# Down products by quadrants, and weight sums by adding transfers, in a two-layer hybrid on one core

## The chip, the cores and the metric

The kernel runs on one core of one Trainium2 chip. A core has TensorE (PE in the profile), VectorE (DVE), ScalarE (ACT), GpSimd (POOL) and SyncE (SP), each with its own in-order instruction stream. The metric is the device time of one execution in microseconds, the median over the runs. The profile is of one execution.

## The reference

Two layers over 512 tokens of width 1024. The first layer mixes by chunked spatial gating and memory attention, the second by forgetting attention and memory attention; each is followed by a gated feed-forward block, which is what the change touches. D_FF is 2816, that is 22 tiles of 128 hidden rows.

```python
def rmsnorm(x, g):
    xf = x.astype(jnp.float32)
    y = xf * lax.rsqrt(jnp.mean(xf * xf, axis=-1, keepdims=True) + RMS_EPS)
    return (y * g.astype(jnp.float32)).astype(x.dtype)
...
for layer in range(DEPTH):
    ...
    h = h + rmsnorm(mixed @ w_out[layer], ln_mix_post[layer])
    f = rmsnorm(h, ln_ffn_pre[layer])
    f = (jax.nn.silu(f @ w_ffn_gate[layer]) * (f @ w_ffn_up[layer])) @ w_ffn_down[layer]
    h = h + rmsnorm(f, ln_ffn_post[layer])
```

Everything is float32.

## The kernel before, in words

**Three matmuls for one product.** A float32 operand is split into a high part (a cast on ScalarE to float32r, line 239) and a low part (a subtraction on VectorE, line 240). `mm3` (line 180) then multiplies high by high, high by low and low by high into the same PSUM tile; these are the lines 182 to 184 of the profile. So every weight tile costs one cast on ScalarE and one subtraction on VectorE (`split`) before TensorE can use it. The parts lie in a ring of eight buffers for high and eight for low parts (`pair_of_parts`, line 123), each of 512 columns.

**Gate and up products.** The hidden row tiles are worked off in pairs. For a pair, `Seven` computes the gate (and then the up) rows of both tiles for all 512 tokens as one 2 by 2 product of blocks: two row tiles by two halves of the depth, times two halves of the depth by two halves of the tokens. Seven block products take the place of eight (the Winograd form of Strassen's scheme). One such `Seven` is called a set here: two weight loads of 512 KB into two of four `raw` buffers of 1024 columns, four sums of 512 columns on VectorE in place (lines 1022 to 1027), seven splits, seven products of twelve 256-column matmuls each (84 matmuls), and evacuations of `x`, `p` and `q` from PSUM into `s1` and `s2` by ScalarE copies (lines 1040 to 1055) and VectorE additions (1060, 1061, 1063). The gate's rows are multiplied by the inverse norm and go through Silu (1110, 1111); the up rows are multiplied by the gate (1116, 1118) and split into `fhi` and `flo`, the form in which the down products read them. The token side was combined and split once, ahead of the loop.

**PSUM.** Gate sets use the three banks of tag `mm`, up sets the three banks of `lg`, so that two sets can overlap.

**Down products.** Row tiles 0 and 1 are computed and multiplied by the down weights first. The other 20 go in four groups, (2 to 8), (8 to 14), (14 to 18) and (18 to 22). After the sets of a group come its down products: for each half `dh` of the 1024 outputs, four PSUM tiles (one per 128 tokens) are accumulated over the group's row tiles, with the hidden rows as the stationary side and 512 weight columns moving, and are then added into the sums `ys` by VectorE (line 1174). For four row tiles this is 4 x 2 x 4 x 3 = 96 matmuls. The last group's down products belong to the tail of the layer (`tail_of`), where the norm is formed.

**Order.** The kernel is written with a tile framework that orders each engine's instructions by its own estimates and takes care of buffers and semaphores. `behind(*last_sum)` ties instructions of a block behind the last evacuations of the set before (the two entries of `last_sum`), on the engine of each. SyncE issues the weight loads in its own order and waits for a free buffer ahead of each load. GpSimd computes the few reciprocal roots and some masks, and issues four small transfers between the layers.

The changed parts are `Seven`, `sevens` (which runs the two sets of a pair), and the loop of `feed_forward`. The core of the loop before:

```python
for dh in range(2):
    outs = [ps("mm" if tb < 2 else "lg", s="y") for tb in range(TB)]
    for kp in range(nk // 2):
        with behind(*(last_sum if dh + kp else ())):
            w = down_weights(layer, k0 + 2 * kp, dh)
```

## Time and profile before

| | |
|---|---|
| median of 3 runs | 1113.62 us (1113.4 to 1114.18) |
| span of the profiled execution, first to last instruction | 1111.4 us |
| TensorE busy | 1100.8 us (99%), 7382 matmuls |
| VectorE busy | 893.7 us (80%), 1735 instructions |
| ScalarE busy | 660.5 us (59%), 1397 instructions |
| GpSimd busy | 25.3 us (2%) |
| transfers | 118.12 MB, mean 106 GB/s |
| mean granted TensorE clock | 0.998 |

The profiled execution's own time is not listed beside its span; the span is 2.2 us below the median of the runs. In the profile's rows, `out<-in` names the tile written and the tiles read, without buffer numbers; `x` is a count; after the bar stand busy microseconds and the mean nanoseconds of one. Matmul records overlap: a matmul's recorded length is longer than the distance to the next one's start, so times per matmul are read from starts. The same holds, to a lesser degree, for VectorE and ScalarE. `PEclk` is the granted clock in tenths.

### The profile page before, as it was taken

How to read it: one execution, taken by the hardware profiler on the slowest of the kernel's cores; microseconds unless marked ns; L12 is line 12 of the kernel's file. 1: busy time of each engine (PE TensorE's matmuls, PEld its weight loads, DVE VectorE, ACT ScalarE, POOL GpSimd, SP SyncE). 2: the span in 40 equal slices, each digit the busy share in tenths (PEclk: the TensorE clock that was granted, in tenths of full speed). 3: DMA queues.
4: the chain of work that ended last, by engine and by line, in shares of the span. 5: the costliest groups of instructions: out<-in, count | busy, mean ns of one | idle time of the engine just before them, and what ended most of it. 6: DMA issues, size and time to landing. Idle time of an engine off the chain costs nothing.

```text
span 1111.4 us, 19500 instructions
## 1 busy us (share of the span) xinstructions
PE 1100.8 (99%) x7382; PEld 1000.1 (90%) x7382; DVE 893.7 (80%) x1735; ACT 660.5 (59%) x1397; POOL 25.3 (2%) x42
## 2 busy tenths in 40 slices
PE   9999999999999999999999999999999999999997
PEld 7998889998899898998988898889999899899996
DVE  8889658997697597896987898858997697687875
ACT  8776468664365264577665667668665265254553
POOL 0100000000000000001000000000000000000000
PEclk9999999999999999999999999999999999999999
DMA  7522322334133323343322654422224133333222
GB/s 267 162 76 77 98 74 76 115 109 141 57 112 97 117 92 114 97 148 117 104 88 62 173 132 116 131 76 74 79 90 154 62 114 96 101 109 114 77 76 76
DMA packets 64421, 118.12 MB, mean 106 GB/s; under 512 B 5260, under 2 KB 40088, under 8 KB 64328
## 3 DMA queue, kind: packets, MB, share of 16 engines
q1 hardware_dynamic: 63720, 116.18, 33.4%
q8 instruction: 58, 0.95, 0.4%
q0 software_dynamic: 192, 0.52, 0.2%
q14 instruction: 35, 0.29, 0.1%
q10 hardware_dynamic: 416, 0.18, 0.1%
HBM read 104.71 MB, written 2.10 MB: 96 GB/s over the span
## 4 chain that ended last, share of the span: by engine, by line
PE 94%; ACT 3%; DVE 1%; issue 1%; POOL 0%; DMA 0%; POOLq 0%; DVEq 0%; ACTq 0%
PE y L182 10%; PE y L183 10%; PE y L184 10%; PE a L182 5%; PE a L184 5%; PE a L183 5%; PE x L184 3%; PE e L182 3%; PE e L184 3%; PE e L183 3%; PE x L183 3%; PE x L182 3%; PE ps L184 3%; PE ps L183 3%; PE ps L182 3%; PE v L182 2%
## 5 line engine op out<-in xcount | busy, mean ns | idle before, releaser
L239 ACT CAST whi<-raw 128x512 fp32r<-128x512 f32 x460 | 273.1, 620 | 217.7 <-PE y L184 89.1
L240 DVE TENSOR_TENSOR wlo<-raw,whi 128x512 fp32r<-128x512 f32 x460 | 303.5, 684 | 69.5 <-ACT whi L239 67.8
L182 PE MATMUL y<-whi,fhi 128*128 128x512 f32 (+1 forms) x356 | 140.2, 394 | 0.4 <-DVE y L838 0.4
L184 PE MATMUL y<-whi,flo 128*128 128x512 f32 (+1 forms) x356 | 139.3, 391 | 0.0
L183 PE MATMUL y<-wlo,fhi 128*128 128x512 f32 (+1 forms) x356 | 139.2, 391 | 0.0
L184 PE MATMUL x<-xshi,wlo 128*128 128x256 f32 x320 | 89.9, 281 | 0.0
L182 PE MATMUL a<-xshi,whi 128*128 128x256 f32 x320 | 89.8, 281 | 0.0
L183 PE MATMUL x<-xslo,whi 128*128 128x256 f32 x320 | 89.7, 280 | 0.0
L182 PE MATMUL x<-xshi,whi 128*128 128x256 f32 x320 | 89.7, 280 | 0.0
L183 PE MATMUL a<-xslo,whi 128*128 128x256 f32 x320 | 89.7, 280 | 0.0
L184 PE MATMUL a<-xshi,wlo 128*128 128x256 f32 x320 | 89.6, 280 | 0.0
L184 PEld LDWEIGHTS y<-whi,flo 128*128 128x128 f32 x356 | 66.8, 188 | 15.7
L182 PEld LDWEIGHTS y<-whi,fhi 128*128 128x128 f32 x356 | 66.8, 188 | 15.6 <-DVE y L838 0.7
L183 PEld LDWEIGHTS y<-wlo,fhi 128*128 128x128 f32 x356 | 66.9, 188 | 14.7
L182 PEld LDWEIGHTS a<-xshi,whi 128*128 128x128 f32 x320 | 60.2, 188 | 0.5
L183 PEld LDWEIGHTS a<-xslo,whi 128*128 128x128 f32 x320 | 60.2, 188 | 0.3
L184 PEld LDWEIGHTS x<-xshi,wlo 128*128 128x128 f32 x320 | 60.3, 188 | 0.0
L183 PEld LDWEIGHTS x<-xslo,whi 128*128 128x128 f32 x320 | 60.2, 188 | 0.0
L184 PEld LDWEIGHTS a<-xshi,wlo 128*128 128x128 f32 x320 | 60.2, 188 | 0.0
L182 PEld LDWEIGHTS x<-xshi,whi 128*128 128x128 f32 x320 | 60.2, 188 | 0.0
L183 PE MATMUL ps<-xslo,whi 128*128 128x256 f32 x192 | 53.9, 283 | 0.6 <-DVE xslo L240 0.6
L184 PE MATMUL ps<-xshi,wlo 128*128 128x256 f32 x192 | 54.4, 285 | 0.0
(297 smaller groups left out, 3111.1 us busy)
## 6 DMA issues: line engine op xcount, KB each, us to landing
raw<-in_w_gate SPq DMA_DIRECT2D x44, 512.0 KB, 3.5
raw<-in_w_up SPq DMA_DIRECT2D x44, 512.0 KB, 3.6
raw<-in_w_down SPq DMA_DIRECT2D x44, 512.0 KB, 3.8
raw<-in_w_out SPq DMA_DIRECT2D x16, 512.0 KB, 4.8
raw<-in_w_b_q SPq DMA_DIRECT2D x8, 512.0 KB, 3.4
raw<-in_w_a_u SPq DMA_DIRECT2D x6, 512.0 KB
raw<-in_w_v SPq DMA_DIRECT2D x6, 512.0 KB, 4.3
raw<-in_w_k SPq DMA_DIRECT2D x6, 512.0 KB
```

What stands on the lines that cost most here:

```text
L182: PE.matmul(o, w[0], x[0], start=start, stop=False, skip_group_check=more)
L183: PE.matmul(o, w[0], x[1], start=False, stop=False, skip_group_check=more)
L184: return PE.matmul(o, w[1], x[0], start=False, stop=stop, skip_group_check=more)
L239: last_hi[0] = A.copy(hi, src)
L240: last_split[0] = last_hi[0], (eng or V).tensor_sub(lo, src, hi)
```

## The change

**Down products as seven.** The groups become (2, 6), (6, 10), (10, 14), (14, 18) and (18, 22). In the first four, that is for 16 of the 22 row tiles, the down product of four row tiles is computed as two 2 by 2 block products (one for each pair of row tiles), summed in PSUM: two row tiles by two halves of the outputs, times two halves of the tokens by two row tiles. The seven products `p`, `q` and `x` are accumulated over both pairs and given out to the quadrants of `ys` by fourteen additions (`give`); `p` is accumulated further after some of its values were given out. `seven_forms` forms the combinations of hidden rows that the products need. Each `Down` loads its weights into two `raw` buffers and a fourth quarter in `a22`, and takes seven splits and two sums. The half `dh = 1` of `ys` is held with its sign turned (`scale=1.0 - 2 * dh`, `turned_sign`).

**Place.** The down products of a group no longer follow its last set. They are kept in `pending` and run after the gate set of the next group's first pair, ahead of that pair's up set; the loads of that up set are issued ahead of the last down product (`ahead`). They use all six banks of `mm` and `lg`.

**Sums by adding transfers.** A set of gate or up weights used to load two times 512 KB and form four sums on VectorE. Now `both` gets the left halves of the two weight tiles, and a transfer from GpSimd's queue adds the whole second tile onto it (`accum_op=ALU.add`), which gives two of the four sums. The other two stay on VectorE. The fourth quarter comes by a load of its own into `a22`. The first three sets of a layer are made without the adding transfer (`adding = m + n > 4`). `Down` uses the same device. A set's seven products are ordered 1, 7, 6, 2, 5, 4, 3 in place of 1, 7, 2, 6, 4, 3, 5, and product 3 accumulates into `p` (but not in the first pair, `late`), so that the last 512-column sum from PSUM becomes one of 256 columns.

```diff
@@ tail_of
-                V.tensor_add(y, o[:, cols], y)
-                junk = temp("sq", (P, T), "sq", 3, BF16)
+                (V.tensor_sub if turned_sign and dh else V.tensor_add)(y, o[:, cols], y)
+                junk = temp("sq", (P, T), "sq", 1, BF16)
@@ class Seven
-        def __init__(self, xs, src, tag, rows):
-            self.xs, self.rows = xs, rows
-            w1, w2 = loaded(src(0)), loaded(src(1))
-            self.a = [w[:, d : d + 512] for w in (w1, w2) for d in (0, 512)]
...
+        def __init__(self, xs, w, m, tag, rows, adding=True, late=False):
+            self.xs, self.tag, self.rows, self.adding, self.late = xs, tag, rows, adding, late
+            raw, both = raw_tile(), raw_tile()
+            self.a11, self.a12 = raw[:, :512], raw[:, 512:]
+            self.s3, self.t = both[:, :512], both[:, 512:]
+            self.a22 = temp("a22")
+            if adding:
+                nc.sync.dma_start(both.rearrange("p (a c) -> p a c", a=2),
+                                  w[m : m + 2, :, :512].rearrange("a p c -> p a c"))
+                nc.sync.dma_start(raw, w[m])
+                G.dma_start(both, w[m + 1], accum_op=ALU.add)
+            else:
+                nc.sync.dma_start(raw, w[m])
+                nc.sync.dma_start(self.s3, w[m + 1, :, :512])
+            nc.sync.dma_start(self.a22, w[m + 1, :, 512:])
@@ sums
-            self.s3 = temp("s3")
-            V.tensor_add(self.s3, a11, a21)
-            self.w1 = self.parts(a11)
-            V.tensor_add(a21, a21, a22)
-            self.w2 = self.parts(a12)
-            V.tensor_add(a11, a21, a11)
-            V.tensor_add(a12, a11, a12)
+            if not self.adding:
+                V.tensor_add(self.t, self.s3, self.a22)
+                V.tensor_add(self.s3, self.a11, self.s3)
+            self.w1 = self.parts(self.a11)
+            self.w2 = self.parts(self.a12)
+            V.tensor_add(self.a11, self.t, self.a11)
+            V.tensor_add(self.a12, self.a11, self.a12)
@@ run
             elif what == 2:
                 self.product(self.x[:, left], self.w2, 2)
+                if not self.late:
+                    V.tensor_add(s1[:, left], self.x[:, left], s1[:, left])
...
             elif what == 3:
-                self.product(self.x[:, right], self.parts(a12), 5)
+                self.product(self.p, self.parts(self.a12), 5, True)
+                last_sum[0] = A.copy(s1[:, right], self.p)
             elif what == 4:
-                self.product(self.q, self.parts(a22), 4, True)
+                self.product(self.q, self.parts(self.a22), 4, True)
+                last_sum[1] = V.tensor_add(s2[:, left], self.q, s2[:, left])
             elif what == 5:
-                self.product(self.p, self.parts(a21), 6, True)
-                last_sum[0] = A.copy(s1[:, right], self.p)
+                self.product(self.p, self.parts(self.t), 6, True)
+                A.copy(s1[:, right], self.p)
+                V.tensor_add(s2[:, right], s1[:, right], s2[:, right])
@@ sevens
+                if n and pending:
+                    pending.pop()()
                 u = make()
                 u.sums()
-                for n in (1, 7, 2, 6, 4, 3, 5):
+                for n in (1, 7, 6, 2, 5, 4, 3):
                     u.run(n)
@@ new
+    def seven_forms(u0, u1, room):
...
+        t = temp("t3", tag="acc", bufs=2)
+        V.tensor_sub(t[:, left], u1[:, right], u0[:, right])
+        V.tensor_sub(u0[:, right], u0[:, left], u0[:, right])
+        pairs = [(act("fhi"), act("flo")) for _ in range(3)]
+        split(u0, *pairs[0])
+        split(u1, *pairs[1])
+        V.scalar_tensor_tensor(out=t[:, right], in0=u0[:, right], scalar=-1.0, in1=u1[:, right],
+                               op0=ALU.mult, op1=ALU.subtract)
+        split(t, *pairs[2])
+        V.scalar_tensor_tensor(out=u1[:, left], in0=t[:, right], scalar=-1.0, in1=u1[:, left],
+                               op0=ALU.mult, op1=ALU.subtract)
+        split(u1[:, left], *room)
...
+    class Down:
+        def __init__(self, layer, k, forms):
...
+            for x in range(2):
+                nc.sync.dma_start(view(both, x), part(x, 0))
+            nc.sync.dma_start(four(raw), some(0))
+            G.dma_start(four(both), some(1), accum_op=ALU.add)
+            nc.sync.dma_start(a22, part(1, 1))
...
+        def first(self):
+            a11, a12, a21, a22 = self.a
+            self.split(0, a11)
+            self.split(1, self.s3)
+            self.split(2, a12)
+        def others(self, n):
+            a11, a12, a21, a22 = self.a
+            if n == 3:
+                V.tensor_add(a11, a21, a11)
+                self.split(3, a11)
+            elif n == 4:
+                self.split(4, a22)
+            elif n == 5:
+                V.tensor_add(a12, a11, a12)
+                self.split(5, a12)
+            else:
+                self.split(6, a21)
+    def down_sevens(layer, k0, forms, ys, ahead):
+        ds = [Down(layer, k0, forms[0])]
+        ds[0].first()
+        with behind(*last_sum):
+            ds.append(Down(layer, k0 + 2, forms[1]))
+            ds[1].first()
+        p, q, x = ([ps(tag, s=s) for tag in ("mm", "lg")] for s in ("p", "q", "x"))
...
+        for o, n in ((p, 0), (q, 1), (x, 2)):
+            product(o, n, (0,))
+        product(p, 0, (1,))
+        give(p, 0, 0)
+        product(q, 1, (1,))
+        give(q, 1, 1)
+        weights(3)
+        product(p, 3, more=True)
+        give(p, 0, 1)
+        product(x, 2, (1,))
+        give(x, 0, 0)
+        weights(6)
+        product(p, 6, more=True)
+        give(p, 1, 1)
+        weights(4)
+        product(q, 4, more=True)
+        give(q, 0, 1)
+        weights(5)
+        ahead()
+        product(p, 5, more=True)
+        give(p, 1, 0)
@@ feed_forward
-        groups = ((2, 8), (8, 14), (14, 18), (18, 22))
+        groups = ((2, 6), (6, 10), (10, 14), (14, 18), (18, 22))
...
+            pending.append(lambda k0=k0, k1=k1, forms=forms:
+                           down_sevens(layer, k0, forms, ys, lambda: make_ahead(k1, 1)))
```

105 lines of the change are left out of this document (69 added, 36 removed).

## The prediction

> **What bounds the kernel now.** I read the page first: shares by engine, the slices, the chain that ended last.
>
> ```profile
> span 1111.4 us, 19500 instructions
> PE 1100.8 (99%) x7382; PEld 1000.1 (90%) x7382; DVE 893.7 (80%) x1735; ACT 660.5 (59%) x1397; POOL 25.3 (2%) x42
> PEclk9999999999999999999999999999999999999999
> PE 94%; ACT 3%; DVE 1%; issue 1%; POOL 0%; DMA 0%; POOLq 0%; DVEq 0%; ACTq 0%
> ```
>
> TensorE is busy 99% of the span at an undiminished clock and 94% of the chain. VectorE stands second with 80%. So matmuls taken away shorten the kernel only as far as VectorE, which must prepare both parts of every weight, keeps up. I therefore looked for one period of the loop that changes: in layer 0, the two pairs (four sets) of the third group and the down products of its four row tiles. TensorE's timeline gives its borders (start, duration).
>
> ```profile
> 388.62 0.28 PE L182 MATMUL a<-xshi,whi 128*128 128x256 f32 x1
> ...
> 428.24 0.39 PE L182 MATMUL y<-whi,fhi 128*128 128x512 f32 x1
> ...
> 450.54 0.28 PE L182 MATMUL a<-xshi,whi 128*128 128x256 f32 x1
> ```
>
> The period takes 450.54 - 388.62 = 61.92 us: four sets of 84 matmuls in 39.62 (0.118 each, start to start) and 96 down matmuls in 22.30, or 0.2323 each. The 0.39 in the rows is a modelled length that overlaps the next matmul; only the distance counts. The windows of the same period (the whole, its sets, its down part; after the length the busy us of PE, PEld, DVE, ACT and POOL, then clock, DMA share and GB/s), and VectorE's waits in it (total us, times, longest):
>
> ```profile
> 388.60:450.50 61.90, 61.90 (x433) 57.63 (x432) 49.66 (x86) 30.29 (x60) 0.00 (x0) 1.00 0.32 103
> 388.60:428.10 39.50, 39.50 (x336) 39.47 (x335) 31.01 (x54) 21.60 (x44) 0.00 (x0) 1.00 0.33 106
> 428.10:450.50 22.40, 22.40 (x99) 18.16 (x98) 18.65 (x32) 8.69 (x16) 0.00 (x0) 1.00 0.31 96
> ```
>
> ```profile
> DVE wlo L240 <- ACT whi L239: 5.5, 7, 2.1
> DVE s L1060 <- PE e L184: 3.4, 2, 3.2
> DVE s L1061 <- ACT s L1049: 2.8, 1, 2.8
> DVE s L1022 <- DMA raw<-in_w_gate: 0.4, 1, 0.4
> ```
>
> TensorE never idles; VectorE works 49.66 us (80%), ScalarE 30.29, the DMA engines 32%. VectorE's 12.1 us of waits are waits for a TensorE that is behind it (eight pairs of weight buffers are its lead), so they cost nothing now. They are the slack that the change spends.
>
> **The change part by part.** *Fewer matmuls.* Per group of four row tiles 96 down matmuls become 7 products x 2 token tiles x 2 row pairs x 3 = 84 of the same shape: 12 x 0.2323 = 2.79 us less. There are four such groups in each of two layers, all the row tiles that leave the old form, so 8 x 2.79 = 22.3 us is the most to be won, and TensorE's floor per period is 59.1 us. The seven products of a set keep their count and are only reordered.
>
> *VectorE.* Back-to-back distances come from its timeline, since durations overlap there too:
>
> ```profile
> 402.65 0.68 DVE L1026 TENSOR_TENSOR raw<-raw,raw 128x512 f32<-128x512 f32 x1
> 403.25 0.68 DVE L240 TENSOR_TENSOR wlo<-s,whi 128x512 fp32r<-128x512 f32 x1
> ...
> 406.26 0.42 DVE L1060 TENSOR_TENSOR s<-e,s 128x256 f32<-128x256 f32 x1
> 406.60 0.68 DVE L240 TENSOR_TENSOR wlo<-raw,whi 128x512 fp32r<-128x512 f32 x1
> ```
>
> That is 0.60 us for 512 columns and 0.34 for 256. Per group: each of four sets loses two weight sums and its 512-wide sum from PSUM and gains one 256-wide sum (12 x 512 fewer, 4 x 256 more); each of two pairs of row tiles gets the combinations of hidden rows instead of two plain low parts (one 512 and five 256 more, so 2 and 10); each of the two sets of down weights needs seven low parts and two sums where it needed four low parts (10 x 512 more); fourteen additions into the sums take the place of eight (6 x 512 more). The balance is 6 x 0.60 + 14 x 0.34 = 8.4 us more, so VectorE comes to 49.66 + 8.4 = 58.1 us against TensorE's 59.1. The two weight sums moved to transfers are already in this: without that part VectorE would have 8 x 0.60 = 4.8 us more, 62.9, and be the bound outright.
>
> *ScalarE.* Nine more 512-wide casts and four more 256-wide copies per group; by these rows 9 x 0.620 + 4 x 0.368 = 7.1 us, so 37.4 of 59 us. Cost nothing: it stays under 65% in the period. The scaled copy in place of a plain one, and one buffer for `sq` in place of three (its writer is ScalarE alone, in order), cost nothing.
>
> ```profile
> L239 ACT CAST whi<-raw 128x512 fp32r<-128x512 f32 x460 | 273.1, 620 | 217.7 <-PE y L184 89.1 <-PE a L183 38.1 <-DVE raw L1026 28.3
> L1052 ACT COPY s<-a 128x256 f32<-128x256 f32 x40 | 14.7, 368 | 11.1 <-PE a L184 11.1
> ```
>
> *Transfers.* A set, and each pair of down row tiles, moves 512 + 512 + 512 + 256 = 1792 KB where it moved 1024; six per period make the DMA share 0.32 x 1.75 = 0.56, up to 0.7 if the adding ones also read their target. Bandwidth is hidden; latency is the question. A sum now needs a plain load, POOL's issue behind a wait for it, and an adding load. POOL is idle in these stages (share 2%, none in the windows above); behind its wait stand only the next adding transfers. On SyncE's queue the plain loads stand in order behind waits for their slots, so the load of the next set's first weights comes as its slot falls free.
>
> ```profile
> DMA to landing us min/median/max: 3.4/4.0/7.5
> L382 POOL DMA_DIRECT2D memk<-memk x4 | 2.3, 572 | 312.2 <-DVE memk L380 312.2
> memk<-memk POOLq DMA_DIRECT2D x4, 128.0 KB, 2.7
> ```
>
> The first row is that of the 512 KB weight loads. No row shows an adding transfer. From below: POOL's own 128 KB land in 2.7, but at four times the bytes the plain load's 4.0 is the nearer floor; from above: twice 4.0, if reading the target halves it, or 7.5 and more. I take 6.0, the middle between 4.0 and 8.0, since a 512 KB transfer is mostly bytes but also holds a fixed part. The chain is then 4.0 + 0.57 + 6.0 = 10.6 us (8.6 to 12.6; with 7.5 for both loads 15.6).
>
> What covers it: in VectorE's order of the changed kernel, between the last read of a slot and the first use of the sum that comes into it stand, going round one group, 14 x 512 and 4 x 256 (9.8 us, down weights), 18 x 512 (10.8 us, the up set behind them), and 16 x 512 and 6 x 256 (11.7 us, the second up set). A chain of 10.6 is late once, by 0.8 us. The direct load of the up set's first weights has only 5 x 0.60 = 3.0 us between its slot's last read and its first low part, against 4.0 + 0.62 for load and cast: late by 1.6. VectorE is in order, so both waits stop all behind them: the evacuations of the down products and the low parts of the next set. TensorE has up to eight weight pairs of cover, but VectorE has just 1.0 us per period with which to win back a lost lead, so in the long run its sum decides: 58.1 + 0.8 + 1.6 = 60.5 us per period against 61.9.
>
> *The coupling in the down products.* `p` is reused four times, so TensorE must wait for VectorE's addition from it. From the gate's end to the first reuse TensorE has 30 matmuls, 30 x 0.2323 = 7.0 us; VectorE has 11 x 0.60 + 0.34 = 6.9 us of work up to the addition that sets `p` free. This fits with nothing to spare; I count zero to 0.5 us and take zero.
>
> *Sum.* 8 x (61.9 - 60.5) = 11.2 us less. The profiled execution spans 1111.4, the median of the three runs is 1113.62, 2.2 above it; the difference of spans is carried over: 1113.6 - 11.2 = 1102 us.
>
> **Rivals.** *Full saving.* If the adding transfer is as quick as a plain one (chain 8.6) and the eight-pair lead swallows the 1.6, TensorE sets the period: 1113.6 - 22.3 = 1091 us. For it: TensorE idle nowhere now, PEclk full. Against: VectorE would have to run at 98% in order. Chance 0.17.
>
> *The adding chain makes VectorE the bound, and the kernel slower.* Place: the three first uses of a sum. Waits are (L - 9.8) + (L - 10.8) + (L - 11.7) for a chain of L; 58.1 + 1.6 plus these pass 61.9 at L = 11.5, so it decides from there. If the add must read its target through the same engines and takes 8.0, L = 12.6 and the waits are 2.8 + 1.8 + 0.9 = 5.5: 65.2 us per period, 1113.6 + 8 x 3.3 = 1140 us; at L = 12, 1113.6 + 8 x 1.5 = 1126. For it: DMA engines near 0.6 busy, rows up to 7.5; against: share was only 0.32, so transfers seldom queue. Chance 0.35. The Trainium skill, Collectives: The Full Stack, section "The bandwidth ceiling: the fold count and why AG ≠ RS ≠ AR", speaks for this rival: an add inside the DMA engine needs two source reads, and its reducing transfer ran at half the rate of a copying one. No run here shows it yet; by that rule the time would be the 1140 of this rival.
>
> *Nothing gained.* At L = 11.5, or with VectorE losing 1.4 us per period in short waits on ScalarE, the floors cancel: about 1113. Chance 0.08.
>
> **How the numbers follow.** The forecast's case (between 1095 and 1111) has 0.40, the full saving 0.17, nothing gained 0.08, the slower case 0.35. A difference under 0.2% (2.2 us) is not told from none. Faster 0.57, same 0.08, slower 0.35. The range goes from the full saving, 1091, into the slower case, to 1130 (L just over 12), which leaves out about 0.15 above and little below; the forecast's own range is 1095 to 1111.
>
> **What would show it.** POOL's transfers are the software queue (packets, MB, share):
>
> ```profile
> q0 software_dynamic: 192, 0.52, 0.2%
> ```
>
> TensorE 7382 - 96 = 7286 matmuls; that queue's 0.52 MB rising to 0.52 + 50 x 0.524 = 26.7 MB; VectorE's 893.7 us up by about 8 x 8.4 = 67 us. Right: landing of the adding transfers near 6 us, VectorE over 95% busy in a period, TensorE's idle time about 11 us more, most of it ended by VectorE (low parts, additions from `p`). Wrong towards slower: VectorE and ScalarE waiting for transfers of the summed weights, several us per group, and PEclk under 9 if TensorE's gaps become long. Wrong towards 1091: no such waits, a period of 59.1.

## The result, and the profile after

The changed kernel takes 1151.3 us (median of 4 runs, 1148.66 to 1151.99) against 1113.74 for the kernel before on the same chip: a ratio of 1.0333 [1.0318, 1.0347], slower. Forecast was 1102, at most 1130. Where executions of one kernel lie more than 1.5% apart, as in one run below, the ratio is taken from its faster ones.

The page of the changed kernel: busy time of the engines, the clock and the DMA engines' share by slices, the hardware and the software queue, the chain that ended last.

```profile
span 1149.7 us, 19935 instructions
...
PE 1101.0 (96%) x7286; PEld 996.1 (87%) x7286; DVE 970.8 (84%) x1907; ACT 704.4 (61%) x1513; POOL 75.3 (7%) x92
...
PEclk9999999999999999999999999999999998998999
DMA  7522312475856585752323645222556746586532
...
q1 hardware_dynamic: 90728, 129.29, 35.6%
q0 software_dynamic: 13536, 26.74, 14.3%
...
PE 73%; DMA 8%; DVE 8%; ACT 6%; issue 5%; POOL 0%; SPq 0%; POOLq 0%; DVEq 0%; ACTq 0%
```

The 96 matmuls are gone and the 26.7 MB are there. TensorE's share of the chain fell from 94% to 73%; transfers, VectorE and ScalarE have the rest. No engine is full. What TensorE waits for (total us, times, longest) is new; its longest wait in the kernel before, and then the first waits of the changed kernel:

```profile
PE yt L871 <- DVE yg L858: 2.3, 1, 2.3
```

```profile
PE a L182 <- ACT s L1053: 17.2, 9, 3.0
PE a L182 <- ACT s L1072: 11.9, 9, 3.5
PE a L182 <- ACT s L1068: 4.2, 8, 0.9
PE e L182 <- ACT whi L239: 3.0, 3, 1.5
```

Tile `a` is the PSUM tile `p` of a set, and lines 1053, 1068 and 1072 are ScalarE's copies out of it after products 1, 5 and 6. TensorE waits 33.3 us for copies of 0.37 us by an engine that is busy 61%.

Windows of the changed kernel: one period of layer 0 (from the first down matmul to the next group's), its four sets, its down products, and one period of layer 1. The columns are those of the prediction.

```profile
343.68:408.50 64.82, 60.35 (x421) 55.77 (x420) 58.41 (x105) 35.42 (x74) 5.97 (x6) 1.00 0.68 171
343.68:388.99 45.31, 40.84 (x337) 39.99 (x336) 39.38 (x75) 26.93 (x58) 5.11 (x5) 1.00 0.77 191
388.99:408.50 19.51, 19.51 (x86) 15.78 (x85) 19.03 (x31) 8.49 (x16) 0.87 (x1) 1.00 0.49 126
946.17:1015.60 69.43, 63.05 (x421) 58.49 (x420) 58.88 (x105) 35.60 (x74) 5.97 (x6) 0.95 0.63 162
```

The down products take 19.51 us, as their 84 matmuls should. The sets, 39.6 us of matmuls, take 45.3 in the one period and 49.9 in the other. So the loss is in the sets, and the six periods between two down parts last 63.9 to 69.4 us.

The timeline of the changed kernel at one late sum of layer 1 (start, duration, engine, in brackets the idle time before and what ended it):

```profile
951.72 0.38 SPq L1015 DMA_DIRECT2D raw<-in_w_up  x1
958.62 0.85 POOL L1018 DMA_DIRECT2D raw<-in_w_up  x1 [7.72 <-DVE wlo L240]
960.78 0.38 ACT L1053 COPY s<-a 128x256 f32<-128x256 f32 x1
...
964.29 0.28 PE L184 MATMUL x<-xshi,wlo 128*128 128x256 f32 x1
966.37 0.62 ACT L239 CAST whi<-raw 128x512 fp32r<-128x512 f32 x1 [5.21 <-issue]
...
967.68 0.37 ACT L1072 COPY s<-a 128x256 f32<-128x256 f32 x1
968.11 0.58 PE L182 MATMUL a<-xshi,whi 128*128 128x256 f32 x1 [3.53 <-ACT s L1072]
968.49 0.41 PE L183 MATMUL a<-xslo,whi 128*128 128x256 f32 x1
968.70 0.41 PE L184 MATMUL a<-xshi,wlo 128*128 128x256 f32 x1
```

The plain load goes out at 951.72. By the trace's semaphore records it lands at 958.06, after 6.34 us; GpSimd issues the adding transfer 0.56 us later, at 958.62, and the sum lands at 966.31, after another 7.69 us. ScalarE's cast of the sum starts at 966.37, so the chain up to the cast is 14.65 us where the prediction had 10.6. This is one of the longest: over all adding transfers the medians from the plain load's issue to the sum's landing are 12.2 us (up sets), 12.7 (gate sets) and 11.5 (down weights), of which the plain load has 5.6, 6.7 and 4.5. ScalarE stands 5.21 us at this cast, and the cast begins 0.06 us after the sum's landing, so it is the sum that ScalarE waits for. Over the whole kernel 32 of ScalarE's casts begin within 0.2 us of the landing of an adding transfer, after 86.6 us of idle time in all. The profile's list of ScalarE's waits has about half of that in a row that names no releaser:

```profile
ACT whi L239 <- issue: 47.1, 19, 5.2
```

The copy of `p` (967.68), which has nothing to do with the sum, is behind it in ScalarE's order, and the next product needs `p` empty. Then the matmuls start 0.21 us apart in place of 0.118. Two windows a little later show why (columns as above; the granted clock is the third from the end):

```profile
970.00:972.00 2.00, 2.00 (x11) 2.00 (x11) 1.92 (x5) 1.21 (x4) 0.00 (x0) 0.50 1.00 188
974.00:976.00 2.00, 2.00 (x19) 2.00 (x18) 1.86 (x4) 0.81 (x3) 0.00 (x0) 0.96 0.00 0
```

After 3.53 us of idle time the granted clock was 0.50 for some 6 us. The Trainium skill, TensorE: Matmul & The Clock Gate, Part 1: The HAM clock gate, says that the array drops to half its clock after an idle window of about 3.4 us and needs as long a busy one to return. This place agrees with the first, but the down products and sets have four more such stretches, and they came after idle times of 2.11, 2.65, 2.88 and 2.99 us, while one of 2.41 us was followed by none. The five stretches at half clock lasted about 3 us in three places and about 6 in two. So here idle times well under 3.4 us are not safe.

Laid over all matmul starts of both kernels, the distances beyond the regular 0.118 and 0.2323 us come to about (the first row has the start and the end of the span in it):

| distance beyond the regular one | before | after |
|---|---|---|
| places of more than 0.25 us | 10.4 us in 9 | 55.2 us in 46 |
| matmuls at half clock | 0 | 9.0 us in 95 |
| smaller ones | 20.2 us | 26.3 us |

That is 59.9 us more, less the 22.3 us of matmuls saved: 37.6, and the spans differ by 38.3.

### The profile page after: what moved, and what is told of

The parts are those of the page before. It is cut to its first block, busy times and chain, and to the rows that moved or that the text cites. A ratio compares the mean times of both kernels' runs of the same rounds, so it can differ in the third digit from the quotient of the medians.

```text
span 1149.7 us, 19935 instructions
## 1 busy us (share of the span) xinstructions
PE 1101.0 (96%) x7286; PEld 996.1 (87%) x7286; DVE 970.8 (84%) x1907; ACT 704.4 (61%) x1513; POOL 75.3 (7%) x92
## 3 DMA queue, kind: packets, MB, share of 16 engines
q0 software_dynamic: 13536, 26.74, 14.3%
## 4 chain that ended last, share of the span: by engine, by line
PE 73%; DMA 8%; DVE 8%; ACT 6%; issue 5%; POOL 0%; SPq 0%; POOLq 0%; DVEq 0%; ACTq 0%
DMA raw<-in_w_up 6%; PE a L182 6%; PE a L184 5%; PE a L183 5%; PE y L182 4%; PE y L183 4%; PE y L184 4%; DVE wlo L240 3%; PE ps L184 3%; PE ps L183 3%; PE ps L182 3%; PE e L184 2%; PE e L182 2%; PE e L183 2%; PE p L184 2%
## 5 line engine op out<-in xcount | busy, mean ns | idle before, releaser
L182 PE MATMUL a<-xshi,whi 128*128 128x256 f32 x464 | 133.7, 288 | 16.0 <-ACT s L1072 11.9
L183 PE MATMUL a<-xslo,whi 128*128 128x256 f32 x464 | 131.3, 283 | 0.0
L182 PE MATMUL a<-d2hi,whi 128*128 128x256 f32 x160 | 47.9, 300 | 17.2 <-ACT s L1053 17.2
L182 PE MATMUL ps<-xshi,whi 128*128 128x256 f32 x192 | 53.7, 287 | 0.0
L182 PE MATMUL y<-whi,mixedhi 128*128 128x512 f32 x128 | 51.6, 403 | 0.0
L183 PE MATMUL y<-wlo,mixedhi 128*128 128x512 f32 x128 | 50.5, 395 | 0.0
L182 PE MATMUL p<-whi,fhi 128*128 128x512 f32 x128 | 50.5, 395 | 0.0
L184 PE MATMUL p<-whi,flo 128*128 128x512 f32 x128 | 50.5, 394 | 0.0
L184 PE MATMUL y<-whi,mixedlo 128*128 128x512 f32 x128 | 50.5, 394 | 0.0
L183 PE MATMUL p<-wlo,fhi 128*128 128x512 f32 x128 | 50.4, 394 | 0.0
```

Of the source, the lines that this page charges most:

```text
L182: PE.matmul(o, w[0], x[0], start=start, stop=False, skip_group_check=more)
L183: PE.matmul(o, w[0], x[1], start=False, stop=False, skip_group_check=more)
L184: return PE.matmul(o, w[1], x[0], start=False, stop=stop, skip_group_check=more)
```

## The experiments

All ratios are against the kernel before on the same chip. Theories named in the expectations: A, the weight sums come late (adding transfers, and their load on the DMA engines), and an in-order engine passes the delay on to TensorE; B, VectorE is too full; C, the new product order costs by itself.

**Without the addition.** Only the addition in the transfer is left out, so the output lacks it. Each engine's instructions stand in the same order as in the changed kernel, so this pair is the cleanest of all.

```diff
-                G.dma_start(both, w[m + 1], accum_op=ALU.add)
+                G.dma_start(both, w[m + 1])
-            G.dma_start(four(both), some(1), accum_op=ALU.add)
+            G.dma_start(four(both), some(1))
```

> The adding transfers of sets and Down objects become plain loads of the same bytes on the same queue with the same waits; the sums are therefore not formed (the buffer holds the second weight tile), so this kernel leaves that addition out. It takes from the adding transfer only what the adding costs the DMA engines (by the profile's shares 26.74 MB in 14.3% of the span, 6.1 us of one engine's sixteenth per 0.01 MB against half of that for plain loads). Theory A with the add's double cost as its main part: TensorE's waits for the copies fall by half or more, 1115 to 1135. Theory A with the serial chain (load, then issue, then second load) as its main part: 1138 to 1150. Theories B and C: unchanged, 1148 to 1153.

(The 6.1 us in this text are per MB, of all 16 engines: 14.3% of 1149.7 us over 26.74 MB.)

Measured: 1105.67 us (1100.48 to 1110.95), ratio 0.9926 [0.99, 0.9952], faster than any of the three ranges. The adding costs 46 us, more than the whole loss. ScalarE's idle time ahead of casts that begin at a landing falls from 86.6 to 31.6 us, in 21 places, and TensorE's largest wait for a copy from 17.2 us to

```profile
PE a L182 <- ACT s L1053: 6.7, 7, 1.6
```

Landing times of GpSimd's transfers, first in the changed kernel (KB each, median us):

```profile
raw<-in_w_up POOLq DMA_DIRECT2D x18, 512.0 KB, 6.4
...
raw<-in_w_gate POOLq DMA_DIRECT2D x16, 512.0 KB, 5.5
...
raw<-in_w_down POOLq DMA_DIRECT2D x16, 512.0 KB, 5.9
```

and then without the addition, with the queue's share:

```profile
q0 software_dynamic: 7392, 26.74, 7.9%
...
raw<-in_w_up POOLq DMA_DIRECT2D x18, 512.0 KB, 4.8
...
raw<-in_w_gate POOLq DMA_DIRECT2D x16, 512.0 KB, 4.1
...
raw<-in_w_down POOLq DMA_DIRECT2D x16, 512.0 KB, 4.8
```

Landing grew by 1.1 to 1.6 us. The DMA engines' time per transfer nearly doubled: 14.3% of 1149.7 us over 50 transfers is 3.3 us, 7.9% of 1109.2 is 1.75. The timeline of the same set without the addition:

```profile
924.33 0.38 SPq L1015 DMA_DIRECT2D raw<-in_w_up  x1
930.71 0.53 POOL L1018 DMA_DIRECT2D raw<-in_w_up  x1 [7.20 <-DVE s L1065]
936.57 0.62 ACT L239 CAST whi<-raw 128x512 fp32r<-128x512 f32 x1 [3.30 <-PE x L184]
```

Here the chain is 12.24 us. The row names TensorE for the cast's wait, but the sum landed at 936.50, 0.07 us before the cast, so here too the sum came last. In this set the plain load took 5.81 us to land, not the 4.0 of the prediction, with the addition or without (6.34). Over all sets the chain's median falls to 9.8 us (up sets), 10.3 (gate sets) and 10.0 (down weights): 1.5 to 2.5 us less than with the addition. The adding transfer itself has 1.1 to 1.6 us of that, and in the up and gate sets the plain load ahead of it has about as much again (1.6 and 1.4); medians need not add up. How far this second part comes from the DMA engines' time was not separated.

**Which of the adding transfers.** The same edit in the sets alone, and in the down products alone; again the same order on every engine, and the addition left out there.

> Edit: the changed kernel with plain transfers in the sets (34 of 50; the addition left out there), adding ones in the down products; every engine's instructions stand in the same order. All plain is 1105.67 us, all adding 1151.3 us, 46 us apart. If the cost goes by the number of adding transfers: 1120 us (16 of 50 of the 46 us stay). If the sets' alone are late (the waits of the changed kernel stand in the sets): 1104 to 1111 us. If either kind alone stays hidden and only both together crowd the DMA engines: 1104 to 1111 us too, and then the other run tells.

> Edit: the changed kernel with plain transfers in the down products (16 of 50; the addition left out there), adding ones in the sets; the same order on every engine. If the cost goes by number: 1137 us. If the sets' alone are late: 1145 to 1152 us. If only both together crowd the DMA engines: 1105 to 1115 us.

Measured: plain in the sets 1127.62 us (1120.05 to 1133.51), ratio 1.012 [1.0072, 1.0167]. Plain in the down products 1128.28, 1138.5, 1146.6 and 1149.4 us; the ratio, 1.0175 [1.0122, 1.0229], is that of the first two, whose mean is 1133.4. Against 1105.67, the 16 adding transfers of the down products cost 22 us (their share by number is 15) and the 34 of the sets some 28 (by number 31), the latter from two executions that lie 10 us apart. Neither kind is hidden alone; which costs more per transfer is not shown. TensorE's waits with adding transfers in the down products alone, then a place of the timeline there:

```profile
PE a L182 <- ACT s L1053: 22.6, 9, 3.6
```

```profile
305.64 1.31 POOL L1144 DMA_DIRECT2D raw<-in_w_down  x1 [10.60 <-DVE raw L1041]
313.75 0.62 ACT L239 CAST whi<-raw 128x512 fp32r<-128x512 f32 x1 [4.41 <-issue]
314.27 0.37 ACT L1053 COPY s<-a 128x256 f32<-128x256 f32 x1
314.69 0.39 PE L182 MATMUL a<-d2hi,whi 128*128 128x256 f32 x1 [3.34 <-ACT s L1053]
```

The first sum of the down weights is cast by ScalarE in the middle of the gate set before, almost 10 us ahead of the first down matmul (323.42), and the copy after product 1 stands behind it. With adding transfers in the sets alone it is the other two copies (rows of the execution of 1146.6 us; they serve only to name the place):

```profile
PE a L182 <- ACT s L1072: 16.5, 7, 4.0
PE a L182 <- ACT s L1053: 7.8, 7, 3.6
PE a L182 <- ACT s L1068: 4.3, 7, 1.2
```

**ScalarE's order.** What reads a late sum (in the sets the cast, the low part and the two additions, in the down products the splits of the sum and of the quarter after it) is tied behind the copy and the addition after product 5 of the set before, in ScalarE's and VectorE's order. The transfers stay. The framework then put 14% of ScalarE's instructions and 16% of VectorE's at other places.

```diff
+                five = A.copy(s1[:, right], self.p)
+                last_five[:] = [five, V.tensor_add(s2[:, right], s1[:, right], s2[:, right])]
...
+            with behind(*(last_five if self.adding else ())):
+                V.tensor_add(self.a11, self.t, self.a11)
+                if self.adding:
+                    self.w7 = self.parts(self.s3)
...
+            with behind(*last_five):
+                self.split(1, self.s3)
+                self.split(2, a12)
```

> As the changed kernel, adding transfers and all, but the cast and the addition that use a late sum are tied behind the copy and the addition that follow product 5 of the set before, in ScalarE's and VectorE's order. ScalarE then has done the copies out of p before it can be stopped by a late sum. If the loss comes through the copies that stand behind a stopped ScalarE (33 us of TensorE's waits), those waits go, and only the lateness beyond TensorE's own lead is left: 1122 to 1138. If the lateness itself is the loss, TensorE waits for the weights instead: 1145 to 1160.

Measured: 1124.65 us (1122.75 to 1127.17), ratio 1.0101 [1.0078, 1.0124]. 27 of the 38 us come back with the same transfers. The waits for copies of `p` are gone but for 1.5 us; left are

```profile
PE p L182 <- DVE y L1197: 7.4, 8, 1.1
PE e L182 <- ACT whi L239: 4.7, 5, 1.5
```

So most of the loss went through the order in which ScalarE and VectorE meet the late sum; the waits that vanished are ScalarE's copies. The first row is the coupling in the down products: in each of the eight, VectorE stands 1.0 to 2.9 us ahead of the addition that reads the second pair's late sum and begins it within 0.2 us of the landing. With the addition left out as well, and every engine's order as in this run:

> Edit: the kernel with the sums behind product 5, with plain loads in place of the adding ones (the addition left out). Theory A (every loss is a late transfer that reaches TensorE through an in-order engine): with both the transfer's lateness and ScalarE's order gone, 1094 to 1103 us, near the 1091 us of TensorE's own work. Theory B (VectorE too full: 58 of 59 us of a period): 1104 to 1110 us, no better than plain loads alone (1105.67 us).

Measured: 1106.04 us (1104.34 to 1106.51), ratio 0.9928 [0.9913, 0.9943]: no better than plain loads alone, in the range of the theory of a full VectorE. The four runs make a square: the same change of order brings 27 us back with the adding transfers and nothing without them. So where transfers are in time that order costs nothing, and the new order by itself gains nothing. Periods are an even 60.0 to 60.6 us against a floor of 59.1, with VectorE at 57.21 of 59.98 us in one of them; whether VectorE holds the last us was not shown.

**Sums back on VectorE.** All of them, in sets and down products:

```diff
-                       up_rows if n else gate_rows, m + n > 4, m == 2)
+                       up_rows if n else gate_rows, False, m == 2)
...
+            V.tensor_add(self.s3, a11, a21)
+            V.tensor_add(a21, a21, a22)
```

> No adding transfer at all: sets and Down objects form all weight sums on VectorE; the down products by quadrants and the order of the products stay. This is the first part of the change alone. Theory A: no waits on transfers are left, VectorE has 58.4 + 12 x 0.60 = 65.6 us per period and is the bound: 1113.7 + 8 x 3.7 = 1143, range 1130 to 1150; so the adding transfers would cost about as much as they save. Theory B: 1151 + 8 x 7.2 = 1209. Theory C: 1145 to 1155.

Measured: 1143.73 us (1142.99 to 1145.59), ratio 1.0269 [1.0252, 1.0286]. A window of one period:

```profile
343.00:408.40 65.40, 61.48 (x422) 55.58 (x421) 64.61 (x117) 35.45 (x74) 0.00 (x0) 1.00 0.33 98
```

VectorE works 64.61 of 65.40 us, and the time is the 1143 us of theory A. The down products as seven need some relief of VectorE, and without it they lose nearly as much. Half the relief:

> All gate and up sets form their four weight sums on VectorE again (no adding transfer in Seven); the two Down objects of a group keep theirs, and everything else is as in the changed kernel (1151.3 us). Theory A (the late sum: load, GpSimd issue and adding transfer take about 14 us in a period whose DMA engines are 70 to 77% busy; ScalarE stands in order before the cast of the late sum, and the copy out of p that TensorE needs stands behind that cast): ScalarE's waits for transfers in the sets go, TensorE's waits for the copies of L1053, L1068 and L1072 fall from 33 us to under 12, and the time is bounded by VectorE, 58.4 + 8 x 0.60 = 63.2 us per period against 61.9 before: 1113.7 + 8 x 1.3 = 1124, range 1115 to 1135. Theory B (VectorE is simply too full): 4.8 us more per period on the bound engine, 1151 + 8 x 4.8 = 1190. Theory C (only the new order of the products, with one product between two uses of p): unchanged, 1145 to 1155.

> The Down objects form their two sums on VectorE and load their weights plainly as 1 KB pieces; the gate and up sets keep the adding transfers, and the rest is as in the changed kernel. Theory A (the adds' time on the DMA engines makes the sums late): a third of the adds, and the 512-byte pieces of the Down loads, leave the DMA engines; VectorE has 58.4 + 4 x 0.60 = 60.8 us per period. With a late sum still to be met in some sets I expect a period of 62.5: 1113.7 + 8 x 0.6 = 1119, range 1110 to 1132. If the adds of the sets alone are what is late: 1140 to 1155. If nothing but VectorE's load counted: 1113.7 - 8 x 1.1 = 1105.

Measured: sums of the sets on VectorE 1161.83 us (1159.12 to 1166.05), ratio 1.0431 [1.0405, 1.0458]; sums of the down products on VectorE 1170.92 us (1169.03 to 1173.4), ratio 1.0505 [1.0484, 1.0525]. Both missed, slower than either whole. For the first the cause stays open (ScalarE waits 58.9 us behind sums of the down weights). For the second it was followed further: the down sums on VectorE, tied behind product 5, and then the same with the fourth part of the down weights in a tile of its own, so that the load buffer comes free earlier.

```diff
+            nc.sync.dma_start(view(both, 1), part(1, 0))
             nc.sync.dma_start(four(raw), some(0))
-            nc.sync.dma_start(four(both), some(1))
+            nc.sync.dma_start(a22, part(1, 1))
```

> Edit: the kernel with the sums behind product 5 (1124.65 us), with the down products' two sums per pair formed on VectorE from plain loads. The same sums on VectorE without the step behind product 5 took 1170.92 us. Theory A (that run lost its time because ScalarE stood at the cast of a late sum with copies and casts behind it): 1118 to 1130 us, VectorE near full at 61 us of a period. Rival (VectorE's own order: the down sums stand behind the up sets' waiting additions, whatever ScalarE does): 1150 to 1170 us.

> Edit: sums behind product 5; the down products' two sums per pair on VectorE from plain loads, with the fourth part in a tile of its own so that the load buffer is given back as early as in the changed kernel. Theory of the buffer (the 43 us that TensorE waited for the up set's sum came from its load being issued 6 us late): that wait goes, 1175.68 less 43 is 1133, less the waits that the second adding transfer of Down caused before (9 us): 1118 to 1133 us. Rival (VectorE full: 58.4 and 2.8 make 61.2 us of a period, so the late sums wait whatever the loads do): 1150 us or more.

Measured: 1175.68 us (1174.93 to 1179.79), ratio 1.0563 [1.0544, 1.0582], and then 1138.76 us (1137.03 to 1146.56), ratio 1.0241 [1.0199, 1.0283]. TensorE's first wait in the former and in the latter:

```profile
PE e L182 <- ACT whi L239: 41.4, 8, 6.3
```

```profile
PE e L182 <- ACT whi L239: 6.2, 8, 1.5
```

In the former the up set's load went out 14.8 us into the down products (SyncE at 268.86, first down matmul at 254.11), in the changed kernel 8.5 us (266.88 and 258.38). In the latter it went out at 12.2 to 12.5 us, only 2.4 us earlier than in the former, yet the up set's sum landed at 22.3 to 23.0 us in place of 27.2 to 28.7: the adding transfer took less time as well. ScalarE's order was not the cause, since tying it back gained nothing (1170.92 to 1175.68 us). The two figures point to the loads, the late issue of this one and what is in flight beside it, rather than to a full VectorE; but the 6 us of the expectation are not what was undone. Of the 43 us expected 37 came back, and the time lies between the ranges of the two theories.

**The adding alone, with the old down products.** Groups, forms and down products as before; adding transfers and the new product order stay.

> The kernel before with the changed sets alone: adding transfers for two of four weight sums and the new order of the products, but the old groups, the old down products after the last set of a group and no combinations of hidden rows. VectorE is relieved, 49.7 - 4 x 1.5 = about 44 us per four row tiles, and TensorE keeps all its matmuls, so its floor is the time of before. Theory A: ScalarE is still stopped by late sums, but four adds per period and a VectorE with slack leave most of it covered: 1114 to 1126. If the adding transfers hurt only a full VectorE: 1112 to 1115. If they hurt by themselves as in the changed kernel: 1135 to 1150.

Measured: 1123.56 us (1122.81 to 1124.34), ratio 1.0085 [1.0069, 1.0101]. No long wait of TensorE; its weight loads carry it:

```profile
PEld a L182 <- ACT s L1053: 7.3, 29, 1.0
```

The matmul that opens product 6 starts late in 29 places, 0.12 to 0.17 us in 26 of them and 0.75 to 0.96 in three (6.1 us), and the next one 0.1 us late each time (3.1 us): 9.2 us, the whole loss. Product 6 now follows product 1 in `p` with one product between. With the sums tied behind product 5:

> Edit: only the adding transfers and the new product order (the down products as in the kernel before), and in addition the late sum's cast and addition are put behind the copy that follows product 5 of the set before. Without that last step it took 1123.56 us, 9 us over the kernel before, with TensorE busy 99% and no long wait: the starts of its matmuls show about 30 places where product 6 begins 0.2 to 0.3 us late in p, which comes to 9 us. Theory A (ScalarE serves in order, and the late sum's cast stands ahead of the copy out of p): the places vanish, 1114 us (1112 to 1118), and adding transfers are then free. Theory C (the new order gives p too little time whatever ScalarE does): 1122 to 1125. Theory B (VectorE too full) has nothing to say here: VectorE is at 76%.

Measured: 1120.71 us (1119.82 to 1122.28), ratio 1.0063 [1.0048, 1.0078], between the two theories: the order has 2 to 3 us of the 9, and 11 late places are left (4.1 us); whether the new product order has the rest was not separated.

**Other orders.** The old product order in the changed kernel; a product of the second pair moved ahead in the down products (on top of the sums behind product 5); that and product 2 ahead of the late sum.

```diff
-                for n in (1, 7, 6, 2, 5, 4, 3):
+                for n in (1, 7, 2, 6, 4, 3, 5):
```

> The sets' products in the order of before (1, 7, 2, 6, 4, 3, 5), product 3 back into x and the 512-wide last sum back (0.26 us more on VectorE per set); adding transfers and down products stay as in the changed kernel. Two products instead of one now lie between two uses of p, 2.8 us of TensorE's work instead of 1.4. Theory A: the late sum still stops ScalarE for 3 to 5 us, but TensorE has 1.4 us more cover at each copy; of about 36 us lost in the periods 10 to 20 come back: 1130 to 1142. Theory B: slower by 8 x 1.0, about 1159. Theory C: all of it comes back, 1092 to 1105.

> Edit: the kernel with the sums behind product 5 (1124.65 us), and in the down products the third product of the second pair is put between the first product and the one that opens p again, so that VectorE has 2.8 us in place of 1.4 to add p into the result. There TensorE waited 8 times 1.1 us for that addition, with 1.8 us more right before it: 10.5 us. Theory A (the places are late one by one, nothing is full): the wait goes, 1114 to 1116 us. Theory B (VectorE is full, 86% busy over the span and more in these stages): the wait turns up at another place, 1122 to 1126 us.

> Edit: as the run with both products moved in the down products, and in the sets the order 1, 2, 6, 7, 5, 4, 3 in place of 1, 7, 6, 2, 5, 4, 3: product 2 needs only the plain loads, so that the first late sum has 1.41 us more. In the sets of the kernel with the sums behind product 5 TensorE still waited 5.6 us ahead of product 7 and 2.8 us behind product 2. Theory A: 8 us less than the run before it, 1104 to 1110 us, faster than the kernel before. Theory B: as the run before it or slower, 1114 to 1126 us; product 6 now needs two sums of VectorE in a row and may wait in place of product 7.

Measured: 1172.25 us (1160.44 to 1176.14), ratio 1.0504 [1.0447, 1.0561]; 1132.64 us (1131.35 to 1134.52), ratio 1.0169 [1.0154, 1.0185]; 1139.85 us (1134.86 to 1143.14), ratio 1.0225 [1.0191, 1.026]. All slower than what they started from. In the second the wait for `p` stayed (8.3 us in 8) and the one ahead of product 7 doubled (9.2 in 7); in the third, product 6 waits. The last two are slower than either of their theories allowed. The places are not late one by one: with late transfers, a gap closed in one place opened in another. Why the first lost 21 us was not followed.

**Sums on GpSimd,** from plain loads.

> The weights are loaded plainly, and the two sums that the adding transfers gave are formed by GpSimd (512 columns, both inputs in SBUF), for the same sets and for the Down objects; twelve additions per period. The DMA engines are as in the kernel without adding transfers, VectorE has 58.4 us per period. If GpSimd works beside VectorE at 1 to 1.5 us each, nothing is late: 1093 to 1108, the first version faster than before. If VectorE's own two-input instructions are held up while GpSimd reads SBUF, VectorE's instructions get longer in the profile by what GpSimd is busy, 12 x 1.2 = 14 us per period, and the time is 1130 to 1200. The Trainium skill, SBUF — State Buffer, section Who interferes with whom, states the second: a VectorE instruction with two SBUF inputs contends with a GpSimd instruction that reads SBUF.

Measured: 1183.49 us (1182.28 to 1186.35), ratio 1.0627 [1.0607, 1.0647]. Two groups of this kernel (busy, mean ns):

```profile
L240 DVE TENSOR_TENSOR wlo<-raw,whi 128x512 fp32r<-128x512 f32 x492 | 361.6, 757 | 12.0 <-ACT whi L239 11.1
...
L1030 POOL TENSOR_TENSOR raw<-raw,a 128x512 f32<-128x512 f32 x34 | 60.0, 1764 | 340.8 <-DMA raw<-in_w_up 156.9 <-DVE wlo L240 62.0 <-DVE y L1185 35.8
```

VectorE's low parts took 757 ns on average in place of 685 in the changed kernel, and its combined multiply of line 1241 1231 ns in place of 687. The Trainium skill, SBUF — State Buffer, section "Who interferes with whom", says that a VectorE instruction with two inputs in SBUF contends with a GpSimd instruction that reads there; this run agrees. VectorE worked 1051.5 us, more than with all sums its own (1020.7).

**The same bytes once more.** Plain loads, and on the same queue each load once more into a spare place that nobody reads (the addition left out); first free, then tied behind its load.

```diff
+                with behind(sums):
+                    G.dma_start(spare[next(spares)], w[m + 1])
```

> Edit: the plain load in place of the adding one (the addition left out, as in the earlier run of 1105.67 us), and right behind each of them on the same queue the same 0.52 MB once more, into a spare place in memory that nobody reads. The adding transfers took 14.3% of the DMA engines, the plain ones 7.9%; two plain ones come to about the adding one's share, but the sums' landing itself is as in the plain run. Theory of engine time (what costs the 46 us between the two is that the adding transfers hold the DMA engines twice as long, so that the loads around them come late): 1140 to 1155 us. Theory of latency (the prediction's: bandwidth is hidden, only the landing of the adding transfer counts): 1105 to 1112 us.

> Edit: plain loads in place of the adding ones (the addition left out), and behind each of them, tied to it, the same 0.52 MB once more into a spare place that nobody reads. In the untied run three periods of the first layer, with 17 such transfers, took 64.3 us in place of 60.7. Theory of engine time: 64 to 66 us in the periods of both layers, 1135 to 1155 us in all, near the changed kernel's 1151. Theory of latency (the landing of the adding transfer itself): the periods stay near 61 us, 1105 to 1115 us; the loss of the untied run then came from the early transfers in the stages before.

Measured: 1142.76 us (1140.44 to 1144.81), ratio 1.0266 [1.0249, 1.0284], and 1214.59 us (1210.74 to 1217.02), ratio 1.0902 [1.0878, 1.0927]. Neither tells cleanly. In the first all extra transfers had gone out by 460 us, 24 of the 50 even before 201 us, ahead of the periods. So three periods of layer 0 had them (62.4, 63.5 and 66.9 us against 59.7, 61.3 and 61.2), layer 1 none (59.8, 61.4, 60.1), and half of the 29.5 us between the two spans was lost before the first period (14.6 us); that the time fell into the range of the engine-time theory is in good part luck. And the framework reordered: 11% of ScalarE's instructions stand elsewhere in the first, 25% in the second, and the second overshot both theories. That extra bytes nobody waits for lengthen the periods beside them speaks for the DMA engines' time as part of the cost; its size is not shown.

## Why the prediction was wrong

Two steps failed: "Bandwidth is hidden", which made the chain to a sum too short, and "Cost nothing" for ScalarE, which left out the way by which a late sum reaches TensorE. The second was the dearer: its undoing brought 27 of the 38 us back. The rest was about right: with the addition left out the kernel takes 1105.67 us, with 1102 forecast, though its chains of 9.8 to 10.3 us are late by 0.2 us at most in the prediction's own count, which would have given 1098, so the nearness is partly chance.

- *Fewer matmuls:* right. 7286 matmuls, 84 in 19.51 us per down part.
- *VectorE:* right in size, 58.4 and 58.9 us of a period where 58.1 was worked out, and right that without the relief it would be the bound (64.6 of 65.4 us; the prediction's 62.9 left out the four sums of the down weights). Over the span it has 77 us more where 67 was forecast. But it was not the place where the delay was passed on, as the prediction said of it.
- *ScalarE, "Cost nothing: it stays under 65%":* the share held (61%), the step failed. A share says nothing of order. ScalarE serves the casts of late sums and the copies out of `p` in one order, and 33.3 us of TensorE's waits ended with such a copy; tying the late readers behind the copy gave 27 us back.
- *Transfers, "Bandwidth is hidden":* the step that failed first. 0.56 to 0.7 held as a mean of the period (0.68 and 0.63), but the transfers are not spread evenly: 0.77 in the sets of the layer 0 period, and in the stretch of the late sum shown above

```profile
951.70:966.40 14.70, 12.30 (x102) 11.89 (x100) 11.18 (x21) 6.40 (x16) 0.85 (x1) 1.00 0.90 230
```

  it was 0.90. There the plain load took 6.34 us where the row of before has 4.0; over the kernel the medians are 5.6, 6.7 and 4.5 us.
- *The adding transfer:* 6.0 us taken, 6.4, 5.5 and 5.9 measured in the median: right. Between the plain load's landing and GpSimd's issue lie 0.57 us, as taken; the issue itself (0.85 us, 1.28 for the down weights) is part of the landing time. So the chain of 10.6 came to 12.2, 12.7 and 11.5 us mostly by its first term. In the set shown, its 4.05 us above 10.6 up to the cast are 2.3 of the plain load and 1.7 of the adding transfer.
- *What that alone would make:* put into the prediction's own waits, 11.5 us for the down weights and 12.2 for the two up sets give 1.7 + 1.4 + 0.5 = 3.6 us in place of 0.8, so 58.1 + 1.6 + 3.6 = 63.3 us per period and 1113.6 + 8 x 1.4 = 1125 us. This is an estimate, not a run, but it lies inside the range that was forecast; that it is near the 1124.65 us with the late readers tied back may be chance. By the prediction's own sum, then, the mis-sized chain does not explain 1151; the runs put the rest on the order around the late sum.
- *The leads* of 9.8 to 11.7 us were counted up to VectorE's first use. ScalarE takes the sum earlier than it is needed, as in the gate set above, almost 10 us ahead, so the lead that counted for it was shorter; by how much over the kernel was not measured.
- *The coupling in the down products:* zero was right in the changed kernel. It showed (7.4 us) once the sets no longer waited.
- *"Only reordered":* the new product order was counted at nothing; with the adding it came to 9 us, of which the order around the late sum has 2 to 3; the rest was not separated between the two.
- *The rival "adding chain", 1140 us:* the side that came, and its chain of 12.6 us is near the measured ones. But it had the whole excess in the adding transfer, where the plain load has much of it, and it passed the delay on through VectorE's sum alone, where ScalarE's order did most of it. The rule of the Trainium skill, Collectives: The Full Stack, section "The bandwidth ceiling: the fold count and why AG ≠ RS ≠ AR", that an add needs two source reads and ran at half the rate, agrees with this case in the engines' time, 3.3 us for 1.75; the landing did not double with it. That rival's time was 11 us too low; the 9.0 us of half clock are among what it left out.
- *What would show it:* the sign "VectorE and ScalarE waiting for transfers of the summed weights" and slices of PEclk under 9 came as written; "most of it ended by VectorE" did not.

No version tried beats the kernel before. The nearest with a complete output are the adding sets with the old down products (1120.71 us) and the sums behind product 5 (1124.65 us).

## What to carry to other kernels

When a load gets a second stage, size its chain with the DMA engines' share in the very stretch where it runs, not with the landing time of the quiet kernel. Then look in every in-order engine at what stands behind the first instruction that reads the late tile: an engine at 61% can stop TensorE if the copy that frees a PSUM tile stands there, and tying the late reader behind that copy may give back most of the loss. An experiment in a framework that orders by its own estimates compares cleanly only where the order of the instructions stayed the same, or where a second pair of runs with the same two orders shows what the order does by itself.

## What the runs showed of the hardware

- An adding transfer of 512 KB took 3.3 us of all 16 DMA engines, a plain one 1.75; it landed after 5.5 to 6.4 us (medians by kind) in place of 4.1 to 4.8.
- After idle times of 2.1 to 3.5 us, TensorE ran at 0.50 of its clock for about 3 or about 6 us, in five places of the changed kernel's sets and down products; an idle time of 2.4 us was followed by none of it. 95 matmuls at half clock cost 9.0 us there.
- GpSimd's additions of 128x512 took 1.54 to 1.76 us on average by group; with them, VectorE's low parts took 757 ns on average in place of 685.
